# Masked decay rows of a gated delta rule: one broadcast product on VectorE, or two scaled copies on ScalarE

## The chip, the cores and the metric

The kernel runs on one core of one Trainium2 chip. The metric is the time of one execution in device microseconds (us). Engines are called as in the profile: PE (TensorE's matmuls), PEld (its weight loads), DVE (VectorE), ACT (ScalarE), POOL (GpSimd), SP (SyncE, which here issues DMAs).

## The reference

One encoder layer in float32 over 1024 tokens of 1024 channels: an RMS norm, one wide projection, two token mixers (a gated delta rule, GDN, with 8 heads, and a gated linear attention, GLA, with 4), each run over the tokens in both directions, then output projections. The change lies in the GDN's decays. In the reference's words, for one direction and one chunk of tokens:

```
g = cumsum(log a)                        # within a chunk
decay[i, j] = exp(g[i] - g[j])  for j <= i, else 0
lower = strict_lower((k * beta) k^T * decay)
u, w  = solve (1 + lower) [u, w] = [v * beta, k * beta * exp(g)]
attn  = (q k^T) * decay
per chunk: v_new = u - w S;  o = (q * exp(g)) S + attn v_new
           S = S * exp(g_last) + (k * exp(g_last - g))^T v_new
```

## The kernel before

The kernel works on chunks of 128 tokens: 8 chunks in each of 2 directions make 16 units per head. The program is written head by head, and a scheduler orders each engine's instructions from dependences and from priorities (`at(...)`, `P_HEAD`, `P_Y`, `P_DT`, `P_Z`, `P_FILL`); each engine then works through its list in order. An instruction that waits holds up everything behind it on its engine.

The stages of one GDN head:

- **Projection** (`gdn_project`, tiles `pj_a`): k, q and v of the head as matmuls with 512 columns, in three passes over the high and low parts of float32 operands. The high part `hi_a` of a weight is cast on ACT (L177), the low part is taken on POOL (L181). Then a short convolution on DVE and ACT (L504 to L508) and a SiLU. The head's gate z is projected the same way (`pj_z`) and copied out of PSUM by ACT (`gz`, L281). All projections share two PSUM banks (the pool `pj`), so a new one starts when an earlier one has been copied out. Projections are the filler: they stand far ahead of their use in the order.
- **Decays** (`gdn_decay`): for each unit a masked row `xm` is built, mask[j, i] times the token's log decay, and a matmul with a strict triangle (`pd`, L585) turns it into sums over tokens. The log decay comes as a high and a low part (`lgh`, `lgl`), so a `pd` bank of four chunks takes four tiles `xm` of two chunks each. There are two `xm` buffers. ACT takes the exponential (`dt`, L588), POOL masks it (`causal`). A head has 16 `xm` tiles, 16 `pd` matmuls and 4 exponentials.
- **Inverse** (`gdn_inverse`): key products (`pgr`, L624), their product with the decays on DVE (`um`, L629), copies into a packed layout (`ul`, L636 on ACT and L638 on DVE), then a substitution over blocks of 32 rows: 120 small DVE instructions (`tmp`, L652, and `yl`, L654), each waiting for the one before. The last of it is the transpose `xq` (L662); the matmuls `p` (L683) start the part that puts blocks together.
- **Scan** (`gdn_scan`): 8 steps, both directions side by side. Each step is a chain over engines: `psc` on PE (L779), `r` on DVE (L781), `psc` on PE (L784), `vd` on DVE (L787) and `vn` on ACT (L789), `psc` on PE (L794), the state `S` on DVE (L799).

The decays of head h+1 are written right behind the inverse of head h; the tile `dt` has two buffers, so a head's decays can be made while the head before is still in its inverse. The GLA and the output projections follow the eighth head.

Of the kernel before, what the change touches and what calls it, by code (L numbers as in the profile page):

```python
# [32 lines left out]
# tiles of loaded weights, of their split parts, of x normalised, of padded projections  # L33
WRAW, WSPLIT, XS, XP = 2, 4, 4, 3
# the order in which a head's k, q and v are projected
A_ORDER = (1, 0, 2)
# the tiles of x that GpSimd scales, the weights whose low parts it takes
X_POOL = (1, 3, 5, 7)
LO_POOL = "azqv"
# blocks of the first projection's gates that are loaded ahead, and the head after whose states  # L40
GA_AHEAD, GA_HEAD = 2, 2
# gates computed beside a head's scan
# [6 lines left out]
# places in the schedule's order  # L49
# [8 lines left out]
def const_array():  # L58
    """Masks and the like: they depend on shapes alone."""
# [29 lines left out]
def layer_kernel(  # L89
# [23 lines left out]
    @contextmanager  # L113
    def at(priority):
        """what is emitted here comes in the schedule's order from this place on"""
        before = tc.cur_priority
        tc.cur_priority = priority
        yield
        tc.cur_priority = before
# [16 lines left out]
    def mm3(ps, lh, ll, rh, rl, n):  # L136
        """ps = (lh + ll)^T (rh + rl), summed over n pieces, without ll^T rl, which is
        below float32's last place."""
# [4 lines left out]
    # ------------------------------------------------------------ what lives throughout  # L143
# [16 lines left out]
    # ------------------------------------------------------------ split weights, projections  # L160
    def split(src, hi, lo):
        """src as a float32r pair whose sum is exact"""
        nc.scalar.copy(hi, src)
        nc.vector.tensor_tensor(lo, src, hi.bitcast(F32), op=ALU.subtract)

    def load_w(src, cols, name, g):
        """part of the rows of columns of a weight, [p, k, n], 512 elements of a partition;
        cols: list of (first column, width, place)."""
# [17 lines left out]
    # the weights' blocks in the order of their use: parts of them are loaded ahead  # L186
# [41 lines left out]
    def project_tokens(name, th, evac):  # L228
        """src^T w for half of the tokens: evac(b, psum) takes [128 tokens, (2 chunks, 256)]"""
        ps = [bank(pj, "pj", f"pj_{name}_{b}") for b in range(2)]  # L230
        for g in range(4):
            hi, lo = next_w(name, g)
            for b in range(2):
                for c in range(2):
                    ts = slice((2 * b + c) * P, (2 * b + c + 1) * P)
                    for k in range(2):
                        kk = 2 * g + k
                        for i, (a, w) in enumerate(((hh, hi), (hl, hi), (hh, lo))):
                            # the first product in a bank clears its marks of what is written
# [6 lines left out]
    def piece(ps, hi, lo, src, th, g, kn, cols=slice(0, 512)):  # L246
        """ps += what the g-th kn pieces of the rows bring, for columns of half of the tokens"""
# [7 lines left out]
    def project(name, evac, src=None):  # L255
        """rows of w^T src: evac(th, psum) takes [channels, 512 tokens]"""
# [8 lines left out]
    def in_steps(name, ps, gn):  # L265
        """as project, by quarters of the tokens"""
# [8 lines left out]
    def project_out(name, dst):  # L275
        """a block of channels kept in DRAM"""
# [13 lines left out]
    # ------------------------------------------------------------ constants of the two mixers  # L290
# [23 lines left out]
    def exp_ln_table():  # L314
        """after a function of another table: the one that has both exp and ln"""
# [4 lines left out]
    # ------------------------------------------------------------ h = rmsnorm(x), transposed  # L320
    with tc.tile_pool(name="xpool", bufs=2) as xpool:
# [23 lines left out]
        def scaled(t):  # L345
            """a tile of x normalised, its transpose"""
# [53 lines left out]
    # ------------------------------------------------------------ decays and gates of the scans  # L400
# [6 lines left out]
    def scan_gates(pool):  # L407
# [17 lines left out]
        # [tokens, direction, head, chunk]  # L425
# [19 lines left out]
        # exp of: the sums up to a token, of what is left of the chunk, of the whole chunk  # L445
# [15 lines left out]
    def finish(o_ps, wcol, rs, zs, o, dst, kc):  # L461
        """o * w * rs * zs, to its place in DRAM; zs is overwritten"""
# [5 lines left out]
    def rs_of(sq, pair, lhsT, eps, name, banks):  # L468
        """sq becomes (mean of sq over the channels + eps) ** -0.5; pair: room for sq as a float32r pair"""
# [11 lines left out]
    # ------------------------------------------------------------ gated delta rule  # L481
# [49 lines left out]
    def gla_stacks(pool):  # L531
        """(r, 1) and (w2, b2) as float32r pairs, stacked for (r_hi + r_lo)^T (w_hi + w_lo) without
# [621 lines left out]
```

## Time and profile before

| what | us |
|---|---|
| median of 3 runs | 1590.22 (1585.59 to 1590.51) |
| span of the profiled execution | 1591.5 |
| PE busy in it | 1526.6 (96%) |
| PEld busy | 1283.3 (81%) |
| DVE busy | 928.0 (58%) |
| ACT busy | 673.1 (42%) |
| POOL busy | 201.8 (13%) |

The profile was taken of one execution; its span lies 1.3 us above the median of the runs, inside their spread at the top. The mean granted clock is 0.982 of full speed. The eight GDN heads lie between about 60 and 802 us, some 80 to 84 us a head in the middle; from there on GLA and output projections follow, in which PE is busy throughout. Matmuls overlap in the profile (one of 512 columns is shown with 0.39 us, and the next starts 0.23 us later), so a busy share of PE says only that it was not waiting.

### The profile page before, as it was taken

The page shows a single profiled execution, that of the slowest core. Times are in us where ns is not written, and L with a number is a line of the kernel's source. Part 1 is how long each engine was busy: PE and PEld are TensorE (multiplying, and loading weights), DVE is VectorE, ACT ScalarE, POOL GpSimd, SP SyncE. Part 2 cuts the span into 40 slices and gives each one's busy share as a digit, 9 for nine tenths or more (in the row PEclk, how much of TensorE's full clock was granted, in tenths as well). Part 3 has the DMA queues.
Part 4 walks back from the last instruction along what each step waited for, and adds up shares of the span by engine and source line. Part 5 has one row for each costly group of instructions (what it writes and reads, how often), then busy time and mean ns, then how long its engine had stood idle before and what let it go on. Part 6 is the DMA issues. An engine that isn't in the chain of part 4 may idle for free.

```text
span 1591.5 us, 25255 instructions
## 1 busy us (share of the span) xinstructions
PE 1526.6 (96%) x9622; PEld 1283.3 (81%) x9622; DVE 928.0 (58%) x2467; ACT 673.1 (42%) x1370; POOL 201.8 (13%) x225
## 2 busy tenths in 40 slices
PE   6998999999999999999999999999999999999998
PEld 6877787787878878787778898898888988787887
DVE  5497779979999899887511113314323355445413
ACT  5552535343444545453232325525436355433311
POOL 4242112111112121000000120110100100000000
PEclk9998999999999999998999999999999999999999
DMA  5221102121212121024143331231221335655404
GB/s 168 72 73 34 41 28 86 41 73 35 93 34 71 51 81 47 30 81 133 40 142 94 86 75 38 62 79 34 75 59 41 106 89 190 212 169 175 134 27 157
DMA packets 140882, 133.48 MB, mean 84 GB/s; under 512 B 11147, under 2 KB 114875, under 8 KB 140757
## 3 DMA queue, kind: packets, MB, share of 16 engines
q1 hardware_dynamic: 133282, 117.78, 25.0%
q10 hardware_dynamic: 6840, 12.00, 2.5%
q0 software_dynamic: 640, 2.10, 0.4%
q8 instruction: 75, 1.23, 0.3%
q14 instruction: 45, 0.37, 0.1%
HBM read 101.45 MB, written 30.39 MB: 83 GB/s over the span
## 4 chain that ended last, share of the span: by engine, by line
PE 62%; DVE 11%; DMA 6%; ACT 3%; issue 1%; SPq 1%; ACTq 0%; DVEq 0%
PE pj_t L251 9%; PE pj_y L251 7%; PE pj_v L240 6%; PE pout L141 5%; PE pj_a L251 5%; PE pj_g L251 5%; DVE tmp L652 3%; PE pj_q L251 3%; PE pj_k L251 3%; DVE yl L654 3%; PE pj_z L251 2%; PE po L768 2%; PE psb L946 2%; PE pob L968 2%; PE psc L794 1%; DMA st<-ob_d 1%
## 5 line engine op out<-in xcount | busy, mean ns | idle before, releaser
L251 PE MATMUL pj_a<-hh,hi_a 128*128 128x512 f32 x368 | 151.7, 412 | 0.0
L251 PE MATMUL pj_a<-hl,hi_a 128*128 128x512 f32 x368 | 151.0, 410 | 0.0
L251 PE MATMUL pj_a<-hh,lo_a 128*128 128x512 f32 x368 | 150.5, 409 | 0.0
L251 PE MATMUL pj_t<-hh,hi_t 128*128 128x512 f32 x256 | 103.9, 406 | 2.4 <-ACT gt L281 2.4
L251 PE MATMUL pj_t<-hh,lo_t 128*128 128x512 f32 x256 | 104.4, 408 | 0.0
L251 PE MATMUL pj_t<-hl,hi_t 128*128 128x512 f32 x256 | 104.3, 407 | 0.0
L181 POOL TENSOR_TENSOR lo_a<-raw_a,hi_a 128x512 fp32r<-128x512 f32 x48 | 68.6, 1430 | 235.1 <-ACT hi_a L177 224.9
L789 ACT ACTIVATE vn<-psc,c 128x128 f32<-128x128 f32 x128 | 45.0, 366 | 116.4 <-DVE vd L787 88.8
L652 DVE TENSOR_TENSOR tmp<-ulb,yl 128x54 f32<-128x54 f32 (+13 forms) x480 | 93.3, 235 | 1.3 <-DMA yl<-in_consts_dram 1.2
L654 DVE TENSOR_TENSOR yl<-yl,tmp 128x54 f32<-128x54 f32 (+13 forms) x480 | 90.9, 231 | 0.1
L251 PEld LDWEIGHTS pj_a<-hl,hi_a 128*128 128x128 f32 x368 | 71.1, 193 | 12.6 <-issue 1.0
L251 PEld LDWEIGHTS pj_a<-hh,lo_a 128*128 128x128 f32 x368 | 70.6, 192 | 12.8 <-issue 0.7
L251 PEld LDWEIGHTS pj_a<-hh,hi_a 128*128 128x128 f32 x368 | 70.6, 192 | 12.2 <-issue 0.7
L251 PE MATMUL pj_y<-ob,hi_y 128*128 128x512 f32 x256 | 79.1, 390 | 0.9 <-DVE gb L1073 0.9
L141 PE MATMUL pout<-wo,hh 128*128 128x512 f32 (+1 forms) x272 | 79.7, 377 | 0.0
L240 PE MATMUL pj_v<-lo_v,hh 128*128 128x256 f32 x256 | 72.4, 283 | 0.0
L240 PE MATMUL pj_v<-hi_v,hl 128*128 128x256 f32 x256 | 72.4, 283 | 0.0
L240 PE MATMUL pj_v<-hi_v,hh 128*128 128x256 f32 x256 | 72.4, 283 | 0.0
L181 POOL TENSOR_TENSOR lo_v<-raw_v,hi_v 128x512 fp32r<-128x512 f32 x32 | 41.3, 1290 | 231.9 <-ACT hi_v L177 226.1
L183 DVE TENSOR_TENSOR lo_t<-raw_t,hi_t 128x512 fp32r<-128x512 f32 x32 | 22.0, 689 | 64.1 <-ACT hi_t L177 64.0
L251 PEld LDWEIGHTS pj_t<-hh,hi_t 128*128 128x128 f32 x256 | 49.3, 193 | 12.2 <-ACT gt L281 2.8
L141 PEld LDWEIGHTS pout<-wo,hh 128*128 128x128 f32 x272 | 50.1, 188 | 9.4
(313 smaller groups left out, 4071.3 us busy)
## 6 DMA issues: line engine op xcount, KB each, us to landing
raw_a<-in_w_in_dram SPq DMA_DIRECT2D x48, 256.0 KB
qe<-eg_d SPq DMA_DIRECT2D x16, 512.0 KB
raw_t<-in_w_in_dram SPq DMA_DIRECT2D x32, 256.0 KB
gt_d<-gt SPq DMA_DIRECT2D x64, 128.0 KB
raw_v<-in_w_in_dram SPq DMA_DIRECT2D x32, 256.0 KB
xt<-in_x_dram SPq DMA_DIRECT2D x8, 512.0 KB
raw_z<-in_w_in_dram SPq DMA_DIRECT2D x16, 256.0 KB
z_d<-gz SPq DMA_DIRECT2D x32, 128.0 KB
```

Source lines behind the costliest of these rows:

```text
L141: nc.tensor.matmul(ps, lhsT=a(k), rhs=b(k), start=(s == 0), stop=(s == len(steps) - 1))
L181: nc.gpsimd.tensor_tensor(lo, raw, hi.bitcast(F32), op=ALU.subtract)
L183: nc.vector.tensor_tensor(lo, raw, hi.bitcast(F32), op=ALU.subtract)
L240: nc.tensor.matmul(ps[b][:, c * 256:(c + 1) * 256], lhsT=a[th][:, kk, ts], rhs=w[:, k, :], start=kk == 0 and i == 0 and c == 0, stop=kk == ...
L251: nc.tensor.matmul(ps[:, cols], lhsT=a[:, k, :], rhs=b[th][:, kk, cols], start=kk == 0 and a is hi and b is src[0], stop=kk == KD - 1 and ...
L652: nc.vector.tensor_tensor(tv, ul2[:, i, 0:i].unsqueeze(2).broadcast_to([P, i, w_]), yv[:, i].unsqueeze(1).broadcast_to([P, i, w_]), op=ALU ...
L654: nc.vector.tensor_tensor(yv[:, 0:i], yv[:, 0:i], tv, op=ALU.subtract)
L768: nc.tensor.matmul(po_n(n), lhsT=lhsT, rhs=rhs, start=count[b] == 1, stop=count[b] == len(todo[b]))
L789: nc.scalar.mul(vn[d], pc[d][:, P:2 * P], c1[:, d, n:n + 1])
L794: nc.tensor.matmul(pc[d][:, 2 * P:3 * P], lhsT=ktok[:, ns], rhs=vd[d], start=True, stop=True)
L946: nc.tensor.matmul(p_s[:, :256], lhsT=ktok[:, u], rhs=vt[:, n], start=True, stop=True)
L968: nc.tensor.matmul(po[e][:, j * P:(j + 1) * P], lhsT=a, rhs=b, start=(i == 0), stop=(i == len(todo) - 1))
```

## The change

In `gdn_decay`, one DVE instruction that multiplies the mask, broadcast over two chunks, with two columns of log decays, broadcast over the mask's row, becomes two ACT instructions, each a copy of the mask scaled by one column (one number per partition). The tile, its buffers and the matmul that reads it stay. The file after has the comments left out and is otherwise the same; behind the edit its lines are one higher (L585 is L586).

```diff
                         m = pool.tile([P, 2, P], F32R, tag="xm", name=f"xm{h}_{d}_{g}_{j}_{w_}", bufs=2)
-                        nc.vector.tensor_tensor(m, mask[d].unsqueeze(1).broadcast_to([P, 2, P]),
-                                                src[:, d, h, ns].unsqueeze(2).broadcast_to([P, 2, P]), op=ALU.mult)
+                        for c in range(2):
+                            n = ns.start + c
+                            nc.scalar.mul(m[:, c], mask[d], src[:, d, h, n:n + 1])
                         nc.tensor.matmul(pd[:, 256 * j:256 * j + 256], lhsT=strict_r[d],
                                          rhs=m.rearrange("p u i -> p (u i)"), start=w_ == 0, stop=w_ == 1)
```

The scheduler then orders all engines anew. Three places matter. The first is ACT between the first head's decays and the copies `gz` of the first z projection. Before, with `dt_1375` the decays of the second head:

```order
L177 CAST hi_a_1_0_904<-raw_a_1_0_902 128x512
L281 COPY gz_0_0_932<-pj_z_0_870 128x256
L281 COPY gz_0_1_935<-pj_z_0_870 128x256
L177 CAST hi_a_1_1_1446<-raw_a_1_1_1444 128x512
L281 COPY gz_1_0_938<-pj_z_1_871 128x256
L281 COPY gz_1_1_941<-pj_z_1_871 128x256
L636 COPY ul_1001<-um_974 32x32x8 x4
L588 ACTIVATE dt_1375<-pd_0_0_1376 128x512
```

After, in the same place (`xm_..._14xx` and `dt_1391` belong to the second head, `xm_..._24xx` to the third):

```order
L585 ACTIVATE xm_1_1_0_1_1454<-call,lgl 128x128 x2
L585 ACTIVATE xm_1_1_1_0_1458<-call,lgh 128x128 x2
L585 ACTIVATE xm_1_1_1_1_1462<-call,lgl 128x128 x2
L585 ACTIVATE xm_0_0_0_0_2434<-call,lgh 128x128 x2
L589 ACTIVATE dt_1391<-pd_1_1_1449 128x512
L585 ACTIVATE xm_0_0_0_1_2438<-call,lgl 128x128 x2
L177 CAST hi_a_1_0_920<-raw_a_1_0_918 128x512
L281 COPY gz_0_0_948<-pj_z_0_886 128x256
L281 COPY gz_0_1_951<-pj_z_0_886 128x256
```

The copies `gz` and the cast `hi_a` have moved from before the second head's `ul` and `dt` to behind all of that head's decays and two tiles of the third's.

The second place is PE, at the second head's decays. Before, `pd` matmuls stand among projections (`pj_a`):

```order
L585 MATMUL pd_0_1_1391<-xm_0_1_1_0_1398,strict_110 128x256
L251 MATMUL pj_a_1_0_1442<-hl_94,hi_a_1_1_874 128x512
L585 MATMUL pd_0_1_1391<-xm_0_1_1_1_1401,strict_110 128x256
L251 MATMUL pj_a_1_0_1442<-hh_92,lo_a_1_1_875 128x512
L251 MATMUL pj_a_1_0_1442<-hh_92,hi_a_1_1_874 128x512
L585 MATMUL pd_1_0_1406<-xm_1_0_0_0_1407,strict_111 128x256
```

After, with `pd_..._655` the first head's last decays and `pd_..._1392` the second head's first:

```order
L586 MATMUL pd_1_1_655<-xm_1_1_1_0_664,strict_111 128x256
L586 MATMUL pd_1_1_655<-xm_1_1_1_1_668,strict_111 128x256
L625 MATMUL pgr_0_991<-k_675 128x128 x4
L625 MATMUL pgr_1_1004<-k_675 128x128 x4
L586 MATMUL pd_0_0_1392<-xm_0_0_0_0_1393,strict_110 128x256
L586 MATMUL pd_0_0_1392<-xm_0_0_0_1_1397,strict_110 128x256
```

From the first head's last seven `pd` to the second head's last, PE's list now holds 23 `pd`, the eight `pgr` and no projection; the next one, `pj_a_1_0_1474`, stands behind them.

The third place is DVE at the first head's substitution. Before, `xm` tiles stand between its instructions:

```order
L640 STREAM_TRANSPOSE ulb_1012<-ul_1001 128x1024
L583 TENSOR_TENSOR xm_0_1_1_0_1398<-call,lgh 128x256
L652 TENSOR_TENSOR tmp_31_1_1016<-ulb_1012,yl_1014 128x31
L652 TENSOR_TENSOR tmp_29_0_1022<-ulb_1012,yl_1014 128x29
L583 TENSOR_TENSOR xm_0_1_1_1_1401<-call,lgl 128x256
L654 TENSOR_TENSOR yl_1014<-yl_1014,tmp_31_1_1016 128x31
```

After, the same rows without them:

```order
L641 STREAM_TRANSPOSE ulb_1028<-ul_1017 128x1024
L653 TENSOR_TENSOR tmp_31_1_1032<-ulb_1028,yl_1030 128x31
L653 TENSOR_TENSOR tmp_29_0_1038<-ulb_1028,yl_1030 128x29
L655 TENSOR_TENSOR yl_1030<-yl_1030,tmp_31_1_1032 128x31
L655 TENSOR_TENSOR yl_1030<-yl_1030,tmp_29_0_1038 128x29
```

Counted in the two lists, 308 projection matmuls with 512 columns stand ahead of the first head's first `p` (L683) on PE before, and 187 after. Ahead of the `pm` matmul that ends a head (L473) there are 481 before and 265 after for the first head, 1037 and 1049 for the fourth, 1708 and 1699 for the eighth.

## Rows read from the trace of the kernel before

**Rows 1.** Windows: from:to, length, busy PE, PEld, DVE, ACT, POOL, clock, DMA, GB/s
```profile
95.00:122.00 27.00, 23.17 (x103) 17.80 (x102) 26.93 (x130) 9.69 (x17) 8.95 (x9) 1.00 0.34 96
396.00:563.00 167.00, 158.56 (x1248) 131.85 (x1248) 152.40 (x480) 79.85 (x174) 31.88 (x40) 1.00 0.21 64
840.00:880.00 40.00, 40.00 (x178) 33.14 (x177) 5.54 (x8) 9.78 (x24) 0.00 (x0) 1.00 0.34 95
```
**Rows 2.** What PE waited for, 60 to 760 us: total, times, longest
```profile
PE psc L794 <- ACT vn L789: 9.8, 8, 2.2
PE pd L585 <- DVE xm L583: 8.5, 12, 3.1
PE psc L779 <- DVE S L799: 5.5, 6, 2.2
PE psc L784 <- DVE r L781: 2.6, 4, 0.8
```
**Rows 3.** Timeline of PE: start, length, instruction, idle before and its releaser
```profile
121.01 0.39 PE L585 MATMUL pd<-xm,strict 128*128 128x256 f32 x1 [3.10 <-DVE xm L583]
121.24 0.39 PE L251 MATMUL pj_a<-hh,hi_a 128*128 128x512 f32 x1
...
122.45 0.63 PE L251 MATMUL pj_a<-hl,hi_a 128*128 128x512 f32 x1
122.88 0.63 PE L251 MATMUL pj_a<-hh,lo_a 128*128 128x512 f32 x1
...
143.12 1.00 PE L683 MATMUL p<-xq,um 32*32 32x32 f32 x29 [2.65 <-DVE xq L662]
```
**Rows 4.** Groups of DVE, 60 to 760 us: busy, mean ns, idle before
```profile
L583 DVE TENSOR_TENSOR xm<-call,lgl 128x256 fp32r<-128x256 f32 x64 | 33.7, 527 | 0.3 <-PE pd L585 0.3
...
L583 DVE TENSOR_TENSOR xm<-call,lgh 128x256 fp32r<-128x256 f32 x64 | 32.1, 502 | 10.8 <-PE pd L585 10.2
```
**Rows 5.** Groups of ACT, 60 to 760 us
```profile
L789 ACT ACTIVATE vn<-psc,c 128x128 f32<-128x128 f32 x112 | 39.4, 366 | 101.8 <-DVE vd L787 77.1 <-PE psc L784 15.2 <-DVE tmp L652 5.9
L494 ACT COPY xp<-pj_a 128x512 f32<-128x512 f32 x46 | 26.9, 585 | 32.9 <-PE pj_a L251 32.7
L177 ACT CAST hi_a<-raw_a 128x512 fp32r<-128x512 f32 x42 | 26.0, 619 | 44.8 <-issue 16.4 <-PE pj_a L251 14.7 <-POOL xp L493 7.6
```
**Rows 6.** Timeline of ACT, head 8's scan
```profile
772.09 0.63 ACT L789 ACTIVATE vn<-psc,c 128x128 f32<-128x128 f32 x2 [2.63 <-DVE vd L787]
```
**Rows 7.** Timeline of ACT, heads 1 and 2
```profile
79.52 1.06 ACT L489 ACTIVATE q<-q 128x1024 f32<-128x1024 f32 x1
...
81.89 1.09 ACT L588 ACTIVATE dt<-pd 128x512 f32<-128x512 f32 x2
82.87 1.08 ACT L604 COPY ktok<-pk 128x512 f32<-128x512 f32 x2
...
85.92 1.28 ACT L489 ACT_TABLE_LOAD   x1
87.22 1.06 ACT L489 ACTIVATE v<-v 128x1024 f32<-128x1024 f32 x1
...
93.61 0.65 ACT L281 COPY gz<-pj_z 128x256 f32<-128x256 f32 x2
...
97.29 2.66 ACT L636 COPY ul<-um 32x256 f32<-32x256 f32 x4 [0.64 <-DVE um L629]
```
**Rows 8.** Timeline of DVE, head 1's substitution
```profile
102.82 0.28 DVE L652 TENSOR_TENSOR tmp<-ulb,yl 128x31 f32<-128x31 f32 x2
...
111.12 0.37 DVE L652 TENSOR_TENSOR tmp<-ulb,yl 128x69 f32<-128x69 f32 x2
111.41 0.37 DVE L654 TENSOR_TENSOR yl<-yl,tmp 128x69 f32<-128x69 f32 x2
...
114.96 1.47 DVE L652 TENSOR_TENSOR tmp<-ulb,yl 128x64 f32<-128x64 f32 x2
...
142.36 0.70 DVE L662 STREAM_TRANSPOSE xq<-yq 128x512 f32<-128x512 f32 x1
```

## The prediction

> **What bounds the kernel now.** I read the windows first, to see in which stretches PE has time to give. In the GLA and output stretch PE never waits: 40.00 busy of 40 [rows 1]. Nothing that the change touches lies there, so only the GDN heads can move. In the fourth and fifth head PE is busy 158.56 of 167, DVE 152.40 and ACT 79.85 [rows 1]. So PE idles 8.4 us in two heads, some 34 in eight. That is the ceiling of any gain, since no matmul goes away; a wait also hides the 0.16 by which a matmul's shown length (0.39) exceeds its spacing (121.01 to 121.24, 0.23) [rows 3], which for some 30 waits lifts the ceiling by 5 at most. Second I read what those waits are for [rows 2]: ACT's `vn` 9.8, DVE's `xm` 8.5, DVE's `S` 5.5 and `r` 2.6, 26.4 together. DVE is the engine nearest to full (152.4 of 167, 91%) and holds 16 of them, but the largest single wait is for ACT, which is to get more work.
>
> The shown busy share of PE overstates it: the Trainium skill, "Perfetto Trace Analysis", section "Identifying the Most-Contended Engine", says that matmul busy time is a poor measure and weight loads a better one. By weight loads the heads are at 131.85 of 167, 79%, which would leave 35 us in two heads. But the dense stretch has 33.14 of 40, 83%, with no wait at all, so against what is reachable the heads are 5% short by this measure too, and the trace agrees with the 34 us.
>
> **What it removes.** 128 DVE products, 33.7 + 32.1 = 65.8 us, 8.2 a head [rows 4]. DVE of the two heads falls from 152.4 to about 136, 81%. Between substitution instructions such a product delays the chain.
>
> **What it adds.** 256 ACT copies of 128x128 with a scale per partition. The trace has no such copy from SBUF. The nearest is `vn`, the same shape and scale from PSUM: 366 ns [rows 5]. SBUF as a source costs 34 ns more at 512 columns (619 for the cast against 585 for the copy) [rows 5], so I take 0.40 us for one. Two back to back take 0.63 together, so the second begins 0.26 after the first [rows 6]; with the 0.03 I take 0.29 as spacing and 0.58 for a pair. Bounds: 0.52, if SBUF costs nothing more, and 0.80, if two do not overlap. For 16 pairs that is 9.3 us a head (8.3 to 12.8) and 74 in all; ACT of the two heads goes from 79.85 to 98, 59%. ACT gets more than DVE loses, but has the room on average. What is queued behind a pair on ACT is the casts of weights, the copies that free projection banks, and `vn`; PE waits for all three.
>
> **The second head's decays: a debt.** The order shows one place where ACT has no room. ACT's list from the SiLU of q, which ends at 79.52 + 1.06 = 80.6 [rows 7], to the first `gz` holds 32 pairs (14 of the first head, 16 of the second, 2 of the third), and PE's list there holds no projection. The projection behind needs a bank that `gz` frees. I add ACT's list up: 32 pairs at 0.58, 18.6; 8 exponentials at 1.09 / 2, 4.4; 3 table loads at 1.28, 3.8; `ktok` and the squares, which before lie from 82.87 to 85.92 with one more behind, 3.3; SiLU of v and the square of q, 1.06 each, 2.1; `ul` 2.7; a cast 0.6 [rows 5, 7]. Sum 35.5, so `gz` comes at 116 and not at 93.6 [rows 7]. PE has run out at about 93. Till 116 it has 23 `pd` at 0.23 and the eight `pgr`, some 6.5 us. It idles about 17.
>
> The same result from the other side: `ul` is done after 22 pairs, 5 exponentials and the rest, 12.8 + 2.7 + 3.8 + 3.3 + 2.1 + 2.7 = 27.4, at 108. With a transpose of 1.2 the substitution starts at 109, against 102.8 [rows 8]. Its 120 instructions at 0.29 / 2 take 17.4; a few of them take 1.47 for two and not 0.36 [rows 8], and I allow four of those, 4.4. That gives 131, and the first `p` at 133 against 143.1 [rows 3]. So the first head's inverse ends 10 us earlier, since DVE has no convolutions and no `xm` between. But 187 projections are done by then and not 308: 121 times 0.23 is 27.5. Net 17 behind. Both ways agree, and with pairs at 0.52 or 0.80 the debt is 15 or 24.
>
> A stall also costs clock: after the wait of 3.10 us the spacing of projections went from 0.23 to 0.43 (122.45 to 122.88) [rows 3], half speed, the lower of the two levels. As PE does `pd` and `pgr` in between, I add nothing for one more such stretch; at the rate of that one it would be 2 us.
>
> **What comes back.** From the third head on the order mostly puts two projections between two `pd`: 3 times 0.23 is 0.69 of PE work for each pair of 0.58 on ACT, so `pd` need not wait, and of its 8.5 us [rows 2] about 7 go. `S` and `r` wait for a DVE that is 11% lighter; of their 8.1 [rows 2] I take half, 4. `vn` waits for ACT, whose load rises by a fifth: I leave its 9.8 [rows 2] as it is, with 5 more as the bad end and 5 less as the good, since `vd` on DVE is ahead of it. With fewer stalls some half-speed time goes, 1. Sum 12.
>
> **Sum.** 17 - 12 = 5 us on the profiled 1591.5 gives 1596.5; the median of the runs lies 1.3 below the profile, so **1595**.
>
> **The rivals.**
>
> *DVE sets the pace (faster).* If DVE at 91% is what ends each head's inverse late, and PE's waits, those for `vn` too, follow from it (most idle time of ACT before `vn` ended with DVE's `vd`, 77.1 us [rows 5]), then all 34 us of idle come back and the debt of 17 is paid once: -17, **1573**. For it: the share, and the first head's inverse, which shortens from 40.3 (102.8 to 143.1) to 24. Against it: the inverse of a later head lies beside the scan of the one before and beside filler, and PE waits for `xm`, `S` and `r` together only 16.6 us. The Trainium skill, "Perfetto Trace Analysis", section "Optimizing Scalar/DVE Operations", says that moving work to Scalar may make sense if DVE is saturated; by rows 1 it nearly is in these heads.
>
> *ACT's queue sets the pace (slower).* Its place is `pd`: PE's list is in order, and a pair that takes more than the 0.69 between two `pd` stops PE, filler and all. At 0.80 that is 0.11 times 16 for 7 heads, 12 us; `vn` waits 5 longer behind pairs; the 8.5 of today's `pd` waits go. With the debt 17 + 12 + 5 - 8 = 26, about **1614**; with the debt of dearer pairs it is 7 more. It decides from a pair of about 0.69 us. For it: `vn` is already the largest wait, and 366 is for another source. Against it: the pair of rows 6 overlaps. The Trainium skill, "ScalarE: Activation LUTs", section "Rules for kernel authors", says to multiply on VectorE and not on ScalarE; the trace agrees so far as one product of 256 columns has a mean of about 0.5 [rows 4] and two `vn` take 0.63 [rows 6], so the rule stands behind this rival.
>
> *The debt isn't there.* If the queue at the second head is shorter than I add up (as ACT may run ahead of the SiLU), 5 to 10 of the 17 go and the kernel ends at 1585 to 1590. I count this with the forecast's lower end.
>
> **How the numbers follow.** A difference under 0.3%, 4.8 us (1585.4 to 1595.0), can't be told from no change here. Forecast, debt and return nearly cancel, 1585 to 1602: 0.42, of which 0.24 falls within 0.3%, 0.16 above and 0.02 below. DVE's pace: 0.29, 0.27 of it below and 0.02 within. ACT's pace: 0.29, 0.28 above and 0.01 within. So faster 0.29, the same 0.27, slower 0.44. The likeliest case's own range is 1585 to 1602; for 8 in 10 it reaches to DVE's 1573 and most of ACT's case, **1574 to 1612**.
>
> **What would show it.** The price: the new line on ACT at 0.40 with a spacing of 0.29. The debt: PE nearly idle from about 93 to 116, `gz` at 116, the first `p` at 133. The return: no waits of `pd` in the third to eighth heads, less than 5 us for `S` and `r`, `vn` near 10. If the eighth head ends some 5 us later than before while PE's waits there are half, the sum holds. It is wrong if `gz` comes before 105, if `pd` waits for ACT through all heads, or if PE in the fourth and fifth head goes above 163 of 167 (DVE's pace).

## The result and the profile after

The changed kernel took 1632.01 us (median of 4 runs, 1629.3 to 1635.02) against 1589.44 for the kernel before, on the same chip: ratio 1.0265, 95% interval 1.0236 to 1.0293. It is slower by 42.6 us where 5 were forecast. The profiled execution has a span of 1628.0, 36.5 longer than before's. One execution of a kernel below (idle matmuls ahead of the first `p`) and one of the kernel before took some 2480 us at a granted clock of 0.56, and the ratios and medians given here leave them out.

The windows of the changed kernel (from:to, length, busy PE, PEld, DVE, ACT, POOL, clock, DMA, GB/s), the same stretches as in [rows 1] and the one behind the first:

```profile
95.00:122.00 27.00, 15.63 (x42) 10.54 (x43) 20.13 (x94) 22.62 (x70) 6.36 (x8) 0.56 0.12 31
122.00:143.00 21.00, 18.18 (x202) 15.35 (x201) 13.97 (x66) 4.64 (x11) 1.81 (x2) 0.74 0.22 62
396.00:563.00 167.00, 158.69 (x1213) 131.01 (x1212) 137.55 (x443) 93.49 (x231) 28.56 (x37) 0.96 0.19 58
```

DVE fell from 152.4 to 137.6 in the stretch of two heads and ACT rose from 79.9 to 93.5, near the forecast 136 and 98. PE idles there as long as before (8.3 of 167 against 8.4), and its clock is 0.96 where it was 1.00. (It is the same stretch of time and not quite the same work: the fourth and fifth head now lie from 425 to 603, with PE busy 170.0 of 178.0 at a clock of 0.97.) From 95 to 122 PE has 42 matmuls in place of 103, at a granted clock of 0.56: most of the stretch ran at the lower of the two levels.

What PE waited for, to the end of the heads (total, times, longest), in the changed kernel:

```profile
PE psc L795 <- ACT vn L790: 19.0, 10, 6.7
PE pd L586 <- ACT xm L585: 10.1, 22, 3.2
PE p L684 <- DVE xq L663: 8.7, 3, 4.4
PE psc L785 <- DVE r L782: 4.0, 4, 1.6
PE pj_a L251 <- ACT xp L494: 3.2, 2, 2.3
PE pgr L625 <- ACT pk L609: 2.8, 1, 2.8
PE pj_t L251 <- ACT gt L281: 2.5, 1, 2.5
PE pj_a L251 <- ACT gz L281: 2.3, 1, 2.3
PE psc L780 <- DVE S L800: 2.2, 4, 0.8
```

And in the kernel before, over the same stretch of 60 to 880 us, which is 120 longer than that of [rows 2]:

```profile
PE psc L794 <- ACT vn L789: 11.7, 9, 2.2
PE pd L585 <- DVE xm L583: 8.5, 12, 3.1
PE psc L779 <- DVE S L799: 5.5, 6, 2.2
PE psc L784 <- DVE r L781: 3.7, 5, 1.2
PE p L683 <- DVE xq L662: 3.2, 2, 2.7
```

All rows of this view add up to 56 us after and 37 before, so waits account for 19 of the 36.5. The clock has to do with the rest. The view of the cores gives it as a mean over the span:

```profile
core 0: 1628.0 us, clock 0.969
```

Before it was 0.982 of 1591.5. What the missing share amounts to is 0.018 x 1591.5 = 29 us before and 0.031 x 1628.0 = 50 us after: 22 more. Waits and clock together give 41, a little above 36.5, as some of the slow time lies in stretches where PE waits in any case. The largest is the one ahead of the first projection after the gap:

```profile
95.00:118.30 23.30, 11.96 (x33) 7.65 (x33) 16.43 (x81) 21.37 (x68) 4.29 (x7) 0.57 0.04 12
```

0.43 x 23.3 = 10 of the 22 us are missing there, where `pd` after `pd` waits for a pair from ACT at either clock, so most of them are no loss beside the wait.

The price and the place of the debt came as forecast. The groups of the new instruction:

```profile
L585 ACT ACTIVATE xm<-call,lgh 128x128 fp32r<-128x128 f32 x128 | 44.2, 391 | 12.6 <-PE pd L586 12.2
L585 ACT ACTIVATE xm<-call,lgl 128x128 fp32r<-128x128 f32 x128 | 43.8, 390 | 1.4 <-PE pd L586 1.2
```

One takes 0.39 us (0.40 was taken from [rows 5]). The timeline of ACT at the second head (start, length, instruction, idle before) shows the spacing and the queue:

```profile
114.69 0.69 ACT L585 ACTIVATE xm<-call,lgl 128x128 fp32r<-128x128 f32 x2
115.29 0.68 ACT L585 ACTIVATE xm<-call,lgh 128x128 fp32r<-128x128 f32 x2
116.06 0.60 ACT L589 ACTIVATE dt<-pd 128x512 f32<-128x512 f32 x1
116.55 0.68 ACT L585 ACTIVATE xm<-call,lgl 128x128 fp32r<-128x128 f32 x2
117.13 0.60 ACT L177 CAST hi_a<-raw_a 128x512 fp32r<-128x512 f32 x1
117.64 0.64 ACT L281 COPY gz<-pj_z 128x256 f32<-128x256 f32 x2
```

A pair ends every 0.59 us (0.58 was forecast), and the first `gz` comes at 117.6 (116 was forecast; 93.6 in [rows 7]). PE in the same stretch:

```profile
115.44 0.58 PE L586 MATMUL pd<-xm,strict 128*128 128x256 f32 x1 [0.20 <-ACT xm L585]
118.33 0.79 PE L251 MATMUL pj_a<-hh,hi_a 128*128 128x512 f32 x1 [2.31 <-ACT gz L281]
118.93 0.63 PE L251 MATMUL pj_a<-hl,hi_a 128*128 128x512 f32 x1
...
133.03 1.56 PE L684 MATMUL p<-xq,um 32*32 32x32 f32 x29 [2.83 <-DVE xq L663]
134.36 0.26 PE L684 MATMUL p<-yq,um 32*32 32x32 f32 x1
```

The last projection before started at 89.27; the next comes at 118.33. The first `p` is at 133.03 (133 was forecast; 143.12 in [rows 3]), with 121 projection matmuls fewer done: 27.5 - 10.1 = 17.4 us behind, as worked out. Where the kernel stands at the end of each head can be reckoned in the same way, as the later time less 0.227 for each further projection done: 38 us at the end of the second head, 27 at the third, 28, 36, 24, 36, and 35 at the eighth. (For the first it says nothing, since other matmuls have changed places around it.) So the debt grew to 27 right behind its place and was never repaid. (A single reading is good to some 10 us, since other matmuls change places at later heads too. With every matmul weighed by its spacing in the kernel before, the heads from the third on read 25, 27, 31, 33, 36 and 35: the swings belong to the method, the slow growth does not.)

### The profile page after: what moved, and what is told of

Its sections match the earlier page's. It is cut to its first block, busy times and chain, and to the rows that moved or that the text cites. A ratio compares the mean times of both kernels' runs of the same rounds, so it can differ in the third digit from the quotient of the medians.

```text
span 1628.0 us, 25387 instructions
## 1 busy us (share of the span) xinstructions
PE 1542.6 (95%) x9622; PEld 1292.4 (79%) x9622; DVE 881.1 (54%) x2339; ACT 744.8 (46%) x1626; POOL 193.5 (12%) x225
## 4 chain that ended last, share of the span: by engine, by line
PE 47%; DVE 4%; DMA 4%; ACT 2%; issue 1%; SPq 1%; ACTq 0%; DVEq 0%
PE pj_t L251 9%; PE pj_y L251 7%; PE pj_v L240 6%; PE pout L141 5%; PE pj_g L251 5%; PE pj_k L251 3%; PE pj_q L251 2%; PE pob L969 2%; PE psb L947 2%; PE pc L901 1%; DMA gt_d<-gt 1%; DVE tmp L653 1%; DMA raw_o<-in_w_out_dram 1%; PE po L769 1%; DVE yl L655 1%; DMA st<-ob_d 1%
## 5 line engine op out<-in xcount | busy, mean ns | idle before, releaser
L181 POOL TENSOR_TENSOR lo_a<-raw_a,hi_a 128x512 fp32r<-128x512 f32 x48 | 64.2, 1340 | 279.6 <-ACT hi_a L177 274.8
L653 DVE TENSOR_TENSOR tmp<-ulb,yl 128x54 f32<-128x54 f32 (+13 forms) x480 | 93.6, 235 | 1.8 <-DMA yl<-in_consts_dram 1.6
L795 PE MATMUL psc<-vd,ktok 128*128 128x128 f32 x224 | 46.0, 301 | 19.5 <-ACT vn L790 19.0
L795 PEld LDWEIGHTS psc<-vd,ktok 128*128 128x128 f32 x224 | 34.5, 194 | 35.1 <-ACT vn L790 33.6
L177 ACT CAST hi_a<-raw_a 128x512 fp32r<-128x512 f32 x48 | 29.7, 621 | 66.5 <-PE pj_a L251 29.0
```

What stands on the lines that cost most here:

```text
L177: i = nc.scalar.copy(hi, raw)
L181: nc.gpsimd.tensor_tensor(lo, raw, hi.bitcast(F32), op=ALU.subtract)
L653: nc.vector.tensor_tensor(tv, ul2[:, i, 0:i].unsqueeze(2).broadcast_to([P, i, w_]), yv[:, i].unsqueeze(1).broadcast_to([P, i, w_]), op=ALU ...
L795: nc.tensor.matmul(pc[d][:, 2 * P:3 * P], lhsT=ktok[:, ns], rhs=vd[d], start=True, stop=True)
```

## Experiments

Two kinds of kernels are used. In one the scheduler lists the instructions anew. In the other a recorded list is forced on every engine: each instruction is tied to issue behind the one before it in that list, and only what is named as free is slotted in by the scheduler. All were timed in 5 rounds beside the kernel before. Forcing a list costs nothing that shows by itself: the two rows of idle matmuls (extra ones whose product is not used) in before's list lie within 0.3% of the kernel before. "Waits" is the sum of all rows of PE's waits from 60 to 880 us, "clock" the missing share of the clock times the span; both come from the profiled execution.

```
product made by         list                          median   ratio (95% interval)    waits  clock
DVE (before)            own                           1589.4                              37     29
ACT pairs (after)       own                           1632.0   1.0265 (1.0236-1.0293)     56     50
ACT pairs               before's                      1629.6   1.0246 (1.0224-1.0268)     57     41
DVE                     after's                       1665.2   1.0481 (1.0447-1.0514)     81     53
none                    before's                      1576.9   0.9927 (0.9906-0.9948)     34     20
ACT, one per tile       before's                      1601.6   1.0068 (1.0048-1.0087)     46     21
high DVE, low ACT       before's                      1614.7   1.0154 (1.0125-1.0184)     57     24
ACT pairs               casts, bank copies first      1613.8   1.0152 (1.0135-1.0170)     43     37
DVE                     casts, bank copies first      1633.7   1.0283 (1.0255-1.0311)     58     40
ACT pairs, vn on DVE    casts, bank copies first      1597.8   1.0051 (1.0032-1.0071)     45     29
ACT pairs, vn on DVE    before's                      1654.9   1.0418 (1.0404-1.0432)     75     46
ACT pairs, vn on DVE    own                           1631.9   1.0263 (1.0238-1.0287)     53     54
heads 1, 2 DVE          own                           1640.6   1.0320 (1.0289-1.0352)     55     59
heads 1, 2 ACT          own                           1650.2   1.0386 (1.0363-1.0414)     63     63
ACT pairs, r0h later    after's                       1638.9   1.0315 (1.0302-1.0329)     60     54
ACT pairs, idle matmuls after's                       1632.7   1.0253 (1.0211-1.0295)     53     59
DVE, idle matmuls       before's, first p             1591.4   1.0009 (0.9985-1.0034)     37     22
DVE, idle matmuls       before's, eighth head         1594.7   1.0023 (1.0004-1.0042)     38     27
DVE                     P_DT 9000                     1610.1   1.0115 (1.0081-1.0148)     42     21
ACT pairs               P_DT 9000                     1653.8   1.0399 (1.0373-1.0424)     64     61
```

Waits and clock together, less their 66 of before, follow the span of each profiled kernel less 1591.5 to within 9 us in all rows. (The profile of DVE with P_DT 9000, 1597.0, lies below all of its other runs.)

**The new list or the price of the pairs?** The first two runs cross operation and list. ACT pairs in before's list (the recorded list is a table of positions by engine; it and `_in_order` are left out here):

```diff
     with _tile.TileContext(nc) as tc:
         layer_kernel(tc, *args)
+        # every instruction behind the one before it in the recorded list; the products are free
+        _in_order(tc, nc, _mybir, XM)
```

> The products are the ACT pairs of the change, but every other instruction of every engine stands in the order that it had before; only the pairs are slotted in by the scheduler. Theory O (the loss comes from the new order of the lists, not from the price of the pairs): 1585 to 1597, no stretch of 17 us without projections at the second head, waits of PE for vn near 10. Theory L (ACT's load itself: casts, copies and vn stand behind pairs wherever they are put): 1610 to 1630, waits for vn and pd together above 25.

Measured 1629.6. Theory O, that the new list alone is to blame, is refuted as it stood; the numbers of theory L came. The loss is spread: 14 us behind at the end of the first head, 18 at the second and third, then up to 42 at the seventh. PE waits 19 us for `xm` (and the `dt` behind it) and 21 for `vn`.

DVE products in the changed kernel's list, the same `_in_order` with the other table:

> The reverse: the order of the changed kernel on every engine, but the products are one DVE instruction again, slotted in by the scheduler. Theory O: most of the loss stays, 1612 to 1632, since PE's list still has no projection among the second head's decays and gz still stands behind them. Theory L: 1588 to 1600, since without pairs ACT reaches gz some 18 us sooner and PE's list does no harm.

Measured 1665.2, outside both. The changed kernel's list is worse with the old operation than with the new one, by 33 us, as before's is worse with the new than with the old, by 40. But the pairs take no longer in before's list (1629.6) than in their own (1632.0).

The two runs also tell where the stall at the second head comes from. Here is its stretch with pairs in before's list, and then with DVE's products in the changed kernel's:

```profile
95.00:122.00 27.00, 22.08 (x104) 16.30 (x103) 13.43 (x48) 24.23 (x68) 7.06 (x8) 1.00 0.26 75
95.00:122.00 27.00, 15.11 (x42) 10.02 (x41) 22.29 (x76) 11.91 (x33) 6.75 (x9) 0.59 0.06 20
```

With the pairs and before's list PE has 104 matmuls there at a clock of 1.00. With DVE's products and the changed kernel's list PE has 42 at 0.59, and its next projection starts at 120.6 (118.3 with pairs), though ACT is busy 11.9 of 27 us. So this stall follows the list, in which PE has no projection between the second head's `pd` and `gz` stands behind its decays; it does not need ACT's queue of pairs. The pairs lose nearly as much by another way in before's list: to 122 us PE waits 11.7 us for them at `pd`, three times 2.8 to 5.2, where it waited 5.1 for products.

**What is DVE's relief worth, and what do fewer instructions on ACT cost?** In before's list, no products:

```diff
-                        m = pool.tile([P, 2, P], F32R, tag="xm", ...)
-                        for c in range(2): ...
+                        if (d, 0) not in KEPT:   # once for each direction
+                            ...
+                        m = KEPT[d, 0]
```

> Leaves out the products: two tiles of masked rows are made once and read by all pd matmuls, so all heads and chunks get the same decays. Order of before on every engine, neither DVE nor ACT does the work. It measures what DVE's relief is worth at most. If DVE sets the pace: 1555 to 1572. If PE's waits come from the order and from what else its chain needs: 1580 to 1590 (the pd waits of 8.5 gone, little more).

Measured 1576.9: 12.6 us less, between the two ranges. In this list DVE does not set the pace: even products for nothing give only a third of the 34 us of idle PE, so that rival of the prediction is refuted as far as a list written with the products in it can do so.

One ACT instruction for a tile in place of two, also in before's list (it leaves out the second chunk's own scales, so its results are not those of the reference):

```diff
-                        for c in range(2):
-                            n = ns.start + c
-                            nc.scalar.mul(m[:, c], mask[d], src[:, d, h, n:n + 1])
+                        nc.scalar.mul(m, mask[d].unsqueeze(1).broadcast_to([P, 2, P]),
+                                      src[:, d, h, ns.start:ns.start + 1])
```

> Order of before, but a tile is one ACT copy of 256 columns, scaled by the first chunk's column alone (the second chunk's decays are so computed from the first chunk's): 128 instructions of about 0.50 with a spacing of 0.40 in place of 256 with 0.29. ACT gets 51 us and not 74, and a tile comes each 0.40 and not 0.58. L1: two thirds of the 40 stay, 1612 to 1620. L2: below the 0.45 of two projections, so nearly all comes back, 1590 to 1600.

Measured 1601.6, 12 and not 40 us more: 64 us of work on ACT (0.50 each) where the pairs have 88. After the first head (8 us behind) nothing is added (5 at the eighth). The pace theory L2 fits, but for 1.6 us above its range: back to back, a tile starts every 0.41 us where a pair starts every 0.59, and two `pd` with one projection between them, the commonest case from the third head on, start 0.43 us apart (medians), as before, and 0.57 with pairs. Those 0.14 us come 21 times, 3 us in all, so how the pace comes to cost 28 us more than one copy does is not shown; a smaller load on ACT is not told apart from a quicker tile here.

High parts on DVE, low parts on ACT:

```diff
+                        if w_ == 1:
                             for c in range(2): ...  # nc.scalar.mul
+                        else:
+                            nc.vector.tensor_tensor(m, ...)
```

> Order of before on all engines, the products of the high parts on DVE as before, those of the low parts as ACT pairs: ACT gets half of the added work. Theory L1 (ACT's total load, 40 us lost for 74 us of pairs): about half, 1605 to 1614. Theory L2 (the cadence: PE's list leaves less than a pair's 0.58 between two pd matmuls): high and low tiles are now made side by side, a tile each 0.3 us, so nearly all comes back, 1585 to 1596.

Measured 1614.7, the numbers of L1, but not its reason: the kernel is 19 us behind at the end of the first head and 19 at the eighth. One wait of 12.4 us in the first head (PE for `xm` from DVE) makes most of it. Later heads lose nothing at half the load, so the loss in this list is not in proportion to ACT's load.

**Is the debt a lasting loss?** The changed kernel with casts and bank copies ahead of all else:

```diff
-        i = nc.scalar.copy(hi, raw)
+        with at(0):
+            i = nc.scalar.copy(hi, raw)
...
         for th in range(2):
-            evac(th, ps[th])
+            with at(0):
+                evac(th, ps[th])
```

> The changed kernel with the copies that empty projection banks and the casts of weights at the front of the scheduler's priorities, so that ACT's list takes them ahead of pairs; PE's list then has projections among the second head's decays again. If the debt at the second head is a lasting loss: 17 us and the half-speed time behind it, some 5, come back: 1605 to 1613. If it is made good later anyway: no change, 1628 to 1636. Theory L has vn still at 19 or more, and the time above 1605.

Measured 1613.8. Its ACT at the second head, and its window:

```profile
91.35 0.59 ACT L591 ACTIVATE dt<-pd 128x512 f32<-128x512 f32 x1
91.84 0.36 ACT L283 COPY gz<-pj_z 128x256 f32<-128x256 f32 x1
92.09 0.41 ACT L587 ACTIVATE xm<-call,lgh 128x128 fp32r<-128x128 f32 x1
```

```profile
95.00:122.00 27.00, 25.77 (x127) 19.99 (x127) 18.18 (x55) 26.51 (x80) 9.89 (x12) 1.00 0.24 72
```

`gz` starts at 91.8, PE has 127 matmuls in the stretch and its clock stays at 1.00, though ACT is as full as it can be (26.5 of 27). 18 us come back, with all pairs still on ACT. By the reckoning of the heads this kernel is 3 us behind at the end of the sixth head and 18 at the eighth. In between lies a stretch in which PE's list holds 160 small matmuls of the seventh head's inverse and no projection for 20 us, and only 20 projections in the next 20:

```profile
680.00:720.00 40.00, 34.55 (x234) 26.84 (x234) 26.33 (x34) 25.04 (x55) 3.15 (x3) 0.57 0.19 61
```

PE is idle for only 5.5 us of these 40, and the missing clock is 0.43 x 40 = 17.

The control, the same priorities with the products on DVE:

> The kernel before (products on DVE) with the same change of priorities as in the kernel that came to 1613.8: casts and copies out of projection banks first. If the priorities cost nothing by themselves: 1584 to 1596, and all of the 24 us that are left there are the pairs'. If the earlier casts crowd out the scans: 1600 to 1612, and the pairs cost little once the debt is gone.

Measured 1633.7, above both ranges. So the priorities by themselves cost DVE's kernel 44 us, much of it behind the sixth head too (11 us behind at its end, 30 at the end of the eighth), and under them ACT pairs are the faster by 20. The 24 that were left over in the run above can't be put on the pairs, and the 18 that came back can't be put on the debt alone, as the rest of the list changed with it.

The first two heads' products apart from the rest, each in a list of its own (the other kernel has `h < 2`):

```diff
-                        for c in range(2):
+                        for c in range(2) if h > 1 else ():
                             ...
+                        if not h > 1:
+                            nc.vector.tensor_tensor(m, ...)
```

> The scheduler's own order, with the first two heads' products on DVE as before and the other six heads' as ACT pairs, so that ACT has no queue of 32 pairs at the second head. If the debt there with its half-speed time is the larger part of the loss (26 of 35 us are behind by the end of the third head): 1598 to 1609. If pairs lose about as much in each head: three quarters of 42 stay, 1618 to 1624.

> The other way round: pairs for the first two heads alone. Debt theory: the whole debt, 1608 to 1618, and the same stretch without projections on PE. Loss per head: a quarter of 42, 1597 to 1603.

Measured 1640.6 and 1650.2: both above all ranges, and neither smaller than the whole change. The courses tell more than the sums. With pairs in the first two heads alone the debt is there (46 us behind at the end of the second head, 35 at the third). With pairs from the third head on it is not (1 to 9 ahead through the fourth head), and then the kernel falls behind all the same: 17 at the fifth, 23, 55 at the seventh, 51 at the eighth. The place looks alike in the fourth to the seventh head: a wait for `xp` that ends at 400.6, 501.2, 596.9 and 697.3, and one for `xq` some 3 to 6 us behind it. ACT in the sixth, with pairs in the later heads alone:

```profile
594.71 0.58 ACT L592 ACTIVATE dt<-pd 128x512 f32<-128x512 f32 x1
595.19 0.68 ACT L585 ACTIVATE xm<-call,lgl 128x128 fp32r<-128x128 f32 x2
595.77 0.61 ACT L177 CAST hi_a<-raw_a 128x512 fp32r<-128x512 f32 x1
596.28 1.07 ACT L494 COPY xp<-pj_a 128x512 f32<-128x512 f32 x2
```

and PE:

```profile
594.27 0.38 PE L589 MATMUL pd<-xm,strict 128*128 128x256 f32 x1 [0.20 <-ACT xm L585]
596.92 0.50 PE L251 MATMUL pj_z<-hh,hi_z 128*128 128x512 f32 x1 [2.26 <-ACT xp L494]
...
600.38 1.57 PE L687 MATMUL p<-xq,um 32*32 32x32 f32 x29 [2.26 <-DVE xq L666]
```

The copy that frees a projection bank (`xp`) stands behind a run of pairs, PE has no projection, waits, has then too few of them ahead of `p`, waits again, and runs slow (from 598 to 625 the clock is at its lower level). It is the mechanism of the debt, in a place where the prediction did not look.

**Is it `vn` behind pairs?** `vn` made by DVE:

```diff
-                nc.scalar.mul(vn[d], pc[d][:, P:2 * P], c1[:, d, n:n + 1])
+                nc.vector.tensor_scalar(vn[d], pc[d][:, P:2 * P], c1[:, d, n:n + 1], None, op0=ALU.mult)
```

With casts and bank copies first:

> The changed kernel with casts and bank copies first, and vn made by DVE in place of ACT: 128 instructions of 0.37 leave ACT, as many of about 0.35 come to DVE, which lost 66 us to ACT. Theory V (what is left of the loss is vn behind pairs in ACT's list, since vd on DVE and vn on ACT read one PSUM bank in turn and the next psc matmul waits for the later): 1590 to 1603, no wait for vn on ACT, DVE waits up by a few us. If DVE's own list is the limit: 1612 or more.

Measured 1597.8, in theory V's range, with PE's waits for `vn` at 17.8 (15.0 with it on ACT), now from DVE. In before's list:

> Order of before on all engines, products as ACT pairs, and vn made on DVE in place of ACT, both slotted in by the scheduler. With vn on ACT it was 1629.6. If pairs cost mainly by holding up vn, which PE waits for at each scan step: 1600 to 1612. If they cost by the pace of pd and by the casts behind them: 1620 to 1632.

Measured 1654.9, with 43 us of waits for `vn`, now from DVE. In the changed kernel's own priorities:

> The changed kernel with its own priorities and vn on DVE in place of ACT. If vn behind pairs costs about 16 us, as between 1613.8 and 1597.8 in the other list: 1612 to 1620. If that was the luck of one list: 1625 to 1655.

Measured 1631.9, no change. PE's waits for `vn` fell from 19.0 to 4.8 there, and others rose for it. The 16 us of the first run belong to one list; taking `vn` off ACT does not bring back what the pairs cost.

**A wait in the eighth head.** In the changed kernel PE waits 6.7 us for one `vn`, which stands on ACT behind a cast `r0h` that waits for a DMA (in the kernel before PE waits 1.9 us there). The changed kernel's list with that cast, and the DVE instruction behind it, two `vn` later:

> The changed kernel in its own order, but for one cast on ACT (r0h, which waits for a DMA and held vn of the eighth head for 6.7 us) and the DVE instruction behind it, which come two vn later. If those 6.7 us and the half-speed time behind them are lost for good: 1620 to 1626. If projections of the later stages fill in for them: within 3 of 1632.

Measured 1638.9, slower by 7. What PE waits for from 780 to 880 us there:

```profile
PE psc L795 <- ACT vn L790: 6.8, 3, 5.2
PE pj_t L251 <- ACT gt L281: 6.7, 2, 4.7
```

The wait did not go: the next cast, `r1h`, comes later in its turn and now holds `vn`, and a bank copy waits 5 us for a store to DRAM. Nothing is won from a wait whose cause, the chain of DMAs, has stayed.

**Is the slow clock a cost of its own?** Idle matmuls in PE's starved stretches of the changed kernel's list (a first product of a pair is issued four times; 12 matmuls of 512 columns ahead of the first `p`):

> The changed kernel in its own order, with idle matmuls where PE starves: each first product of a tile pair of the first head's second direction and of the second head is issued four times into the same place (the last counts), and 12 matmuls of 512 columns stand ahead of the first head's first p, overwritten by it. If the clock is a cost of its own that PE's activity keeps away: the half-speed stretches from 95 to 146 (38 us) mostly go, and with them 10 to 19 us: 1613 to 1622. If it does nothing, or the extra matmuls only add work: 1630 to 1640.

Measured 1632.7. The window from 95 to 122:

```profile
95.00:122.00 27.00, 16.54 (x61) 13.62 (x61) 17.65 (x93) 20.66 (x66) 3.46 (x6) 0.50 0.04 10
```

61 matmuls and not 42, yet the clock is 0.50: the added ones did not raise it, and the question is not answered there.

In the kernel before, 11 idle matmuls ahead of the first `p`, in the wait of 2.65 us [rows 3]:

> The kernel before in its own order, with 11 idle matmuls of 512 columns (2.5 us) in the wait of 2.65 us ahead of the first head's first p. If the wait is why the clock is half from 145.7 to 155.9: 5 us less, 1583 to 1586. If it is the small matmuls behind: 1588 to 1592.

PE there:

```profile
139.93 2.65 PE L679 MATMUL p<-hh 128*128 128x512 f32 x11
142.89 1.00 PE L686 MATMUL p<-xq,um 32*32 32x32 f32 x29 [0.31 <-DVE xq L662]
...
145.53 0.39 PE L251 MATMUL pj_z<-hh,lo_z 128*128 128x512 f32 x1
145.76 0.40 PE L251 MATMUL pj_z<-hh,hi_z 128*128 128x512 f32 x1
```

The spacing behind `p` stays at 0.23 where it had been 0.43 from 145.7 to 155.9, and the end of the first head comes 4.6 us sooner. So filling this wait kept the clock up. But the median is 1591.4, no change that can be told: the lead is 4 us to the end of the third head and gone by the fourth, where a new stretch at half clock stands (397 to 407).

The same ahead of the 64x64 products of the eighth head:

> The kernel before in its own order, with six idle matmuls of 512 columns ahead of each of the two 64x64 products of the eighth head, which stand in 17 us at half clock. Full-width matmuls cost 2.7 us and give back up to 8.5 if they lift the clock: 1582 to 1587. If not: 1591 to 1594.

Measured 1594.7, 0.0 to 0.4% slower. The clock was back at 1.00 from 754 and not from 763.5, some 3 us of missing clock less, and the 12 matmuls, 2.7 us, cost about what that gave.

What can be compared is executions of one kernel. Over the 117 timed executions of the 19 kernels besides the one before, each against the mean of its own kernel, 1 us more of missing clock (1 less the clock, times the span) goes with 0.75 us more time (correlation 0.91). So the clock goes with most of its own share of time while the program stays the same; what made it fall in one execution and not in another is not shown.

**How much does another list cost?** One number of the priorities changed in the kernel before, and then in the changed one:

```diff
-P_DT = 12000
+P_DT = 9000
```

> The kernel before, products on DVE, with one number of the priorities changed (decays ahead of the inverse of the head before, P_DT 9000 in place of 12000): the same work in another list. If the list written for before is near its best and others lose by waits and clock: 1605 to 1640. If lists differ little: 1585 to 1596.

> The changed kernel with P_DT 9000 in place of 12000, beside the 1610 that the products on DVE had with it. The second head's gz still stands behind its pairs, so the debt of 17 and its half-speed time stay. If the operation decides: 1640 to 1655, some 40 above 1610. If the list decides: anything from 1605 to 1660, with the difference to 1610 unlike the 43 at 12000.

Measured 1610.1 and 1653.8, the second in the first of its two ranges. The same work in another list costs 20 us; with it the change costs 44, as it did with 12000 (43).

## Why the prediction was wrong

The forecast was 1595 and the time is 1632. The profile's 36.5 us are, about, the debt of 17, then 10 more of waits and 11 more of missing clock behind 122 us, where the prediction expected 12 to come back.

**What bounds the kernel** was right: PE's idle time in the heads. But it was read as the ceiling of a gain, 34 us, and as if nothing else of PE's time could move. Its clock can: behind 122 us its missing share rose as much as the waits did.

**The price of a pair** was right (0.39 and 0.59 against 0.40 and 0.58), from the nearest row and not from the bounds. So was **the debt** in this kernel: its place, its length to 2 us and its size of 17. (PE's list holds 16 `pgr` in the stretch and not eight, which changes nothing, as ACT sets its length.) But it was laid to ACT's queue, and the same stall came with DVE's products in the same list: the list makes it, with either operation.

**"What comes back", 12 us, is the first step that failed.** Nothing came back. Behind 122 us, where the return was to be, these are PE's waits at `pd`, first before, then after:

```profile
PE pd L585 <- DVE xm L583: 3.4, 7, 1.1
PE pd L586 <- ACT xm L585: 1.0, 5, 0.2
```

`pd` did stop waiting in the later heads, as forecast, but that was worth 2.4 us and not 7: the other 5.1 of the 8.5 stood ahead of 122 us, in the place of the debt, where 9.2 stand now. `S` fell by 3 and `r` did not, 2.6 in place of 4. Against this the waits that the sum put at no change or did not price rose: `vn` by 7 (4.8 of it the one wait in the eighth head), `xq` by 5.5, and the copies `xp` by 3. So waits behind 122 us went from 32 to 42. The term looked at `pd`, `S` and `r` as waits for a busy engine, which a lighter DVE would shorten. The run without products shows what that is worth in before's list: 12.6 us, and only if ACT gets nothing in exchange.

**"I add nothing" for the clock is the second.** It was argued that `pd` and `pgr` keep PE at work in the stall. The window shows 0.56, though in the stall itself that cost little, since ACT set the pace. Behind it more stretches at the lower level came (132 to 146, 235 to 242, 266 to 279): 19 us of missing clock from 122 to the end of the third head against 12 in the kernel before, and 38 against 27 to the end of the program. The prediction expected 1 us of such time to go.

**A threshold by luck.** The prediction let a pair take up to 0.69 us between two `pd` with two projections between them. These start 0.59 us apart in the trace (medians, both kernels), since a `pd` takes 0.12 there and not 0.23. A pair at 0.59 just fits.

**The rivals.** DVE's pace is refuted (above). ACT's queue was the right side, not the right size: 1614 (its own sum, 26, gives 1616) against 1632, and by its own condition, a pair dearer than 0.69, it should not have come. Its place was wrong too: in all, PE waits for pairs at `pd` little longer than it did for products (10.1 against 8.5 us); the loss came through what stands behind them, the casts and copies that free projection banks. The prediction named these as queued behind a pair and priced them at one head only. None of its three signs of being wrong came (`gz` early, `pd` waiting through all heads, PE above 163 of 167): no sign watched the clock or `xq`.

**What is shown and what stays open.** Shown: the gap without projections at the second head follows the list (it comes with either operation in the changed kernel's, with neither in before's); the scheduler writes such a list when the first two heads alone have pairs; and the same wait for a bank copy behind pairs comes in later heads when only these have pairs. In the changed kernel the debt is not made good by the eighth head. That the 42.6 us are the debt's and its followers' is argued and not shown: pairs in before's list have no such gap and lose 40 all the same, and the list without it that gained 18 differs in much else. Shown too: the sum of the parts is not the whole. The other lists cost the products on DVE 20, 44 and 76 us; pairs cost 43 and 44 us under two sets of priorities and 40 in before's list, and gain 20 and 33 in two others. What decides which list loses where is open beyond the places named here, and only the run without products was faster than before.

## What to carry to other kernels

When work moves to an engine that has room on average, list what stands behind it on that engine, head by head. Look first for copies that free a bank for the filler of the busiest engine: here work that was made early, a head ahead of its use, stood in front of them. When the engine that sets the end loses its filler, count the clock as well as the wait; a repayment from waits for another engine should be credited only when a run without the moved work shows it. And when a scheduler writes the order, run each operation in the other's list and under more than one set of priorities: here the gap that looked like the price of the operation came with the list, and under one set of priorities the sign of the change turned.

## What the runs showed of the hardware

- PE's clock in the stretch from 95 to 122 us was 1.00 where projections stood among the `pd` (103, 104 and 127 matmuls in three lists). Where the list had none, it fell to 0.56 and 0.59 (42 matmuls), and to 0.50 with idle ones added (61).
- Over 117 executions of 19 kernels, 1 us more of missing clock went with 0.75 us more time within a kernel.
- An ACT copy of 128x256 from SBUF with a column scale took 0.50 us and one of 128x128 0.39; two of the smaller, back to back, 0.68. In a row, tiles of two instructions started every 0.59 us and tiles of one every 0.41.
- A wait of 2.65 us filled with 11 matmuls of 512 columns kept the clock up for the 10 us behind it, which had been at half. The whole kernel did not gain (1591.4 against 1589.4).
